# A hybrid decoder layer on one core: a longer count for an inversion, norm roots with their own rank, and one residual added by the transfer

## The chip, the core and the metric

The kernel runs on one core of a Trainium2 chip. The core has engines with instruction queues of their own: TensorE (PE in the profile) multiplies matrices into PSUM banks, VectorE (DVE) and ScalarE (ACT) work elementwise, GpSimd (POOL) and SyncE (SP) here issue transfers between DRAM and the core's memory. Each engine takes its instructions in the order in which the program has them, and an instruction waits on semaphores for what it reads and for the buffer that it writes. The metric is the device time of one execution in microseconds (us); lower is better.

## What is computed

One layer of a decoder, on 1024 positions of width 1024, in float32. Cut to what matters here:

```python
h = rms_norm(x, norm_mix_pre)
proj = h @ w_in                                # RWKV r,k,v and low ranks | S5 input u | two gates
g_rwkv, g_s5 = jnp.split(jax.nn.sigmoid(gates_of(proj) + b_gate), 2, axis=-1)
o_rwkv = rwkv7_branch(p_rwkv, ...) @ w_branch_rwkv   # delta-rule state, then a norm per head
o_s5 = s5_branch(u_s5, ...) @ w_branch_s5            # diagonal state space, GELU, GLU
mixed = (g_rwkv * o_rwkv + g_s5 * o_s5) @ w_out
x = x + rms_norm(mixed, norm_mix_post)         # the first residual
h = rms_norm(x, norm_ffn_pre)
f = conv_ffn(h, w_up, conv_w, conv_b, w_down)
x = x + rms_norm(f, norm_ffn_post)             # the second residual
```

`rms_norm` multiplies by the reciprocal root of the mean square over the 1024 channels.

## The kernel before

Activations lie transposed: channels on the 128 partitions, positions along the free axis, in tiles of 128x512. The 1024 positions are worked as two halves of 512 (`th` 0 and 1). Every float32 product is three matmuls on a split of both operands into a high and a low part (`mm3_steps`, lines 172 to 174: high by high, low by high, high by low); three such matmuls are a step. Splitting an operand takes ScalarE (the high part, lines 156, 226, 231) and VectorE (the low part, lines 157, 227, 232). Results collect in a few PSUM banks; two of them (`gm`) serve the wide products around the change.

**What sets TensorE's order.** TensorE's instructions stand in the order in which the code is written, and `drive` decides that order while the program is built. Lanes (generators) yield a cost and a delay in estimated us: `prep_lane` (the RWKV half's inputs, its Gram matrices and `rwkv_inv`, the inversion of its triangular blocks), `chain_lane` (`rwkv_level`, then the eight steps of `rwkv_chain` over the state), `out_lane` (`rwkv_out`: norm per head, transposes, gate). A lane that is not ready by the driver's own clock gives way to a stream of filling work (`fill`): `merge` for the first half (gates and GLU, eight tiles of one gate and eight of the other), then `merge_s5` (the S5 side of the second half), then the output projection of the first half, and behind the lanes the norms. The constant `T_INV` is the delay by which the driver counts VectorE's and the transfers' part of an inversion; `T_LN` and `T_LE` are those of the norm in `rwkv_out`, for the first and the second half. A longer delay lets more of the filling work go ahead of what waits, and takes it from what comes later.

**What sets the other engines' order.** VectorE, ScalarE, GpSimd and SyncE are ordered by a scheduler by rank: `high_priority(n)` ranks instructions earlier. `HPW` is used for loads of weights and gate tiles, and `HPN` above that.

**The level of the second half.** `rwkv_inv` ends on VectorE (lines 788, 790) and goes through DRAM and back on POOL's queue (`xd`, line 792; `gr`, line 797). `rwkv_level` transposes `gr` on VectorE (line 811, four instructions), multiplies on TensorE (line 821) and copies on ScalarE (line 825). Beside it run tiles of `merge`. Such a gate tile loads a 128x512 tile `GT` into one of three buffers `ev` (line 1184), makes 12 matmuls into `gm`, and multiplies both on VectorE (line 1192), which frees the `gm` bank; an add (line 1238) and a split (231, 232) free the `ev` buffer. `s5_inputs` (line 1243) loads a tile `YU` into the same three buffers (line 1166), with a Gelu (line 1167), and a cast and a subtraction (226, 227) behind it.

**The norm in `rwkv_out`.** For each of two groups VectorE subtracts a mean, sums squares (ScalarE squares into `ev` buffers for the second half, lines 912 and 913), makes a root (lines 131 to 139) and multiplies (line 916). TensorE transposes the result (line 922).

**The norms behind the mixing sublayer.** `mid_norms` sums squares of the projection's eight tiles `mx`, calls `post_norm` and then norms once more for the next sublayer. `rstd` makes a reciprocal root on VectorE out of nine small instructions (lines 265 and 131 to 139), `spread` brings it to all partitions by TensorE (line 271). `post_norm` loads x into buffers `tx` by SP, multiplies each tile by root and gain (line 1295), adds x (line 1296), squares the sum on ScalarE (line 257), adds up the squares on VectorE (line 259, first half) and stores the sum to DRAM (line 1299, from ScalarE's queue for the first half). At the same time the second half's `merge_rk` runs: its gate tiles load `GT` on POOL's queue (line 1184), and their products are split by lines 231 and 232.

Of the kernel before, what the change touches and what calls it, by code (L numbers as in the profile page):

```python
# [13 lines left out]
ALU = mybir.AluOpType  # L14
# [6 lines left out]
NK = D // 128  # L21
# [45 lines left out]
class Kern:  # L67
# [194 lines left out]
    def rstd(self, ss, eps, scale):  # L262

        v = self.small.tile([128, 4], F32, tag="rv", name=self.nm("rv"), bufs=2)
        self.nc.vector.tensor_scalar(v, ss[:, :4], scale, eps, ALU.mult, ALU.add)
        return self.rsqrt(v, 4, "nr")

    def spread(self, bc, y):

# [1009 lines left out]
    def post_norm(self, src, ss, th, gain, resid, store, squares=None):  # L1279


        nc = self.nc
        o = slice(th * 512, th * 512 + 512)
        xs, sq = [], []
        for k in range(NK):
            xs.append(self.tx())
            nc.sync.dma_start(xs[k], resid(k, o))
        bc = self.rp()
        y = self.rstd(ss, 1e-6, 1.0 / D)
        yield 0, T_RS  # L1290
        self.spread(bc, y)
        yield 0.9, 0
        for k in range(NK):
            y = src[k]
            nc.vector.scalar_tensor_tensor(y, y, self.vec(gain, k), bc, ALU.mult, ALU.mult)
            (nc.vector if k % 2 or squares is not None else nc.gpsimd).tensor_tensor(y, y, xs[k], ALU.add)
            if squares is not None:
                sq.append(self.square_into(sq[-1] if sq and th == 0 else None, y))
                (nc.sync if th else nc.scalar).dma_start(store(k, o), y)
            else:  # L1300
                (nc.sync if th else nc.gpsimd).dma_start(store(k, o), y)
        if squares is not None:
            yield 0, T_N2 if th else T_N5
            for i, x in enumerate(sq if th else sq[-1:]):
                self.sumsq(squares, x, i == 0)
                yield 0.5, T_N4

    def outproj(self, th, mg, mx):

# [556 lines left out]
    def prep_lane(self, g):  # L1866
        for th in range(2):
            yield 0, (lambda: self.masked >= 2 * th + 1 and self.all_in) if g else (lambda: self.chunks >= 14 * th)
            d = self.ds[th][g]
            self.rwkv_tiles(d, g, th)  # L1870
            yield from self.rwkv_front(d, g, th, self.pts[th], (lambda: self.chains >= 1) if th > g else (lambda: self.grams > 2 * th) if g else T_LD)
            self.fronts += 1
            if g:
                yield from self.rwkv_inv(self.ds[th], th)
                yield 0, T_INV
                self.preps += 1

    def chain_lane(self):
# [29 lines left out]
T_LD, T_SQ, T_LT = 6.0, 3.0, 3.5  # L1908
NEVA = 4
T_KN, T_BK, T_GR, T_NF, T_MT, T_INV, T_LV, T_CH = 7.0, 4.0, 4.0, 5.0, 8.0, 43.0, 1.0, 0.8  # L1910
T_LN, T_LE = 32.0, 20.0
T_N0, T_RS, T_N1, T_N2, T_N4, T_N5, T_N3 = 2.5, 4.0, 2.2, 5.0, 1.6, 40.0, 2.0
NET = 5
MGAP = 2
# [17 lines left out]
HPW, HPN = 400000, 500000  # L1932
# [64 lines left out]
```

## Time and profile before

| | |
|---|---|
| runs before | 1499.52, 1508.82, 1509.49 us; median 1508.82 |
| the profiled execution | 1501.13 us; its span 1499.4 us |
| TensorE's granted clock over that span | 0.98 of full |
| TensorE busy | 1436.3 us |
| VectorE, ScalarE busy | 1072.2 us, 730.3 us |
| bytes read and written in DRAM | 150.14 MB, 52.43 MB |

The span runs from the first to the last instruction that the profiler recorded; the execution's own time has the start and the end around it. A row of the timeline gives the start in us, the duration in us, the engine, the line of the code, the operation, the tile written and those read, the shape, and in brackets how long the engine stood idle before it and what ended that. `SPq` and `ACTq` are the queues of SyncE and ScalarE when they issue a transfer. In the list of waits a row reads: who waited for whom, us in total, times, longest.

### The profile page before, as it was taken

How to read it: one execution, taken by the hardware profiler on the slowest of the kernel's cores; microseconds unless marked ns; L12 is line 12 of the kernel's file. 1: busy time of each engine (PE TensorE's matmuls, PEld its weight loads, DVE VectorE, ACT ScalarE, POOL GpSimd, SP SyncE). 2: the span in 40 equal slices, each digit the busy share in tenths (PEclk: the TensorE clock that was granted, in tenths of full speed). 3: DMA queues.
4: the chain of work that ended last, by engine and by line, in shares of the span. 5: the costliest groups of instructions: out<-in, count | busy, mean ns of one | idle time of the engine just before them, and what ended most of it. 6: DMA issues, size and time to landing. Idle time of an engine off the chain costs nothing. (4 is left out here: it accounts for less than half of the span.)

```text
span 1499.4 us, 24150 instructions
## 1 busy us (share of the span) xinstructions
PE 1436.3 (96%) x9284; PEld 1177.0 (78%) x9284; DVE 1072.2 (72%) x1761; ACT 730.3 (49%) x1167; POOL 58.7 (4%) x116
## 2 busy tenths in 40 slices
PE   7999999999999899798999999999999999999996
PEld 5778888788878687576878877888888887888785
DVE  8977774756226859456597799777777777697677
ACT  7677653533324564443455455444444444444351
POOL 0000000010100110100000000000000000000001
PEclk9999999999999999799999999999999999999997
DMA  6453432642512675433365633222222227943723
GB/s 221 124 187 113 131 94 93 203 133 100 170 52 76 189 222 177 135 100 113 117 197 179 204 125 128 84 79 78 83 85 84 85 71 243 322 143 126 229 95 112
DMA packets 121284, 206.26 MB, mean 138 GB/s; under 512 B 29248, under 2 KB 35520, under 8 KB 121168
## 3 DMA queue, kind: packets, MB, share of 16 engines
q1 hardware_dynamic: 113296, 182.43, 37.7%
q0 software_dynamic: 6144, 19.99, 4.0%
q10 hardware_dynamic: 1728, 2.29, 0.4%
q8 instruction: 73, 1.20, 0.3%
q14 instruction: 43, 0.35, 0.1%
HBM read 150.14 MB, written 52.43 MB: 135 GB/s over the span
## 5 line engine op out<-in xcount | busy, mean ns | idle before, releaser
L172 PE MATMUL gm<-hh,wh 128*128 128x512 f32 x672 | 276.6, 412 | 8.0 <-DVE rsy L139 5.1
L173 PE MATMUL gm<-hl,wh 128*128 128x512 f32 x672 | 265.7, 395 | 0.0
L174 PE MATMUL gm<-hh,wl 128*128 128x512 f32 x672 | 265.3, 395 | 0.0
L156 ACT CAST wh<-wf 128x512 fp32r<-128x512 f32 x171 | 105.7, 620 | 186.3 <-PE gm L173 117.8
L157 DVE TENSOR_TENSOR wl<-wf,wh 128x512 fp32r<-128x512 f32 x171 | 117.0, 687 | 91.6 <-ACT wh L156 89.2
L172 PEld LDWEIGHTS gm<-hh,wh 128*128 128x128 f32 x672 | 127.9, 190 | 40.2 <-issue 7.9
L174 PEld LDWEIGHTS gm<-hh,wl 128*128 128x128 f32 x672 | 128.1, 191 | 28.1
L173 PEld LDWEIGHTS gm<-hl,wh 128*128 128x128 f32 x672 | 128.3, 191 | 25.1 <-issue 1.0
L1615 PE MATMUL d<-xl,wh 128*128 128x512 f32 x308 | 120.8, 392 | 3.5 <-DVE xl L227 3.5
L1614 PE MATMUL d<-xh,wh 128*128 128x512 f32 x308 | 120.9, 392 | 2.1 <-ACT xh L226 2.1
L1616 PE MATMUL d<-xh,wl 128*128 128x512 f32 x308 | 120.6, 392 | 0.0
L1440 PE MATMUL rp<-t,h 128*128 128x512 f32 x216 | 84.4, 391 | 2.6 <-ACT p L1454 1.6
L1442 PE MATMUL rp<-t,l 128*128 128x512 f32 x216 | 84.2, 390 | 0.5 <-DVE l L227 0.5
L1441 PE MATMUL rp<-t,h 128*128 128x512 f32 x216 | 84.1, 389 | 0.0
L1615 PEld LDWEIGHTS d<-xl,wh 128*128 128x128 f32 x308 | 58.2, 189 | 16.7 <-DVE xl L227 4.7
L1614 PEld LDWEIGHTS d<-xh,wh 128*128 128x128 f32 x308 | 58.2, 189 | 14.8 <-ACT xh L226 2.5
L1616 PEld LDWEIGHTS d<-xh,wl 128*128 128x128 f32 x308 | 58.1, 189 | 12.1
L226 ACT CAST h<-r 128x1024 fp32r<-128x1024 f32 x34 | 35.8, 1054 | 61.1 <-PE rp L1441 29.6
L227 DVE TENSOR_TENSOR l<-r,h 128x1024 fp32r<-128x1024 f32 x34 | 41.6, 1224 | 29.2 <-ACT h L226 27.7
L1461 DVE SCALAR_TENSOR_TENSOR y<-zv,vecs,y 128x1023 f32<-128x1023 f32 (+1 forms) x36 | 46.1, 1280 | 8.5 <-ACT y L1459 8.5
L1440 PEld LDWEIGHTS rp<-t,h 128*128 128x128 f32 x216 | 40.5, 188 | 12.2 <-ACT p L1454 2.5
L1454 ACT COPY p<-rp 128x512 f32<-128x512 f32 x54 | 31.0, 574 | 37.0 <-PE rp L1442 37.0
(459 smaller groups left out, 3198.5 us busy)
## 6 DMA issues: line engine op xcount, KB each, us to landing
r<-in_w_up_dram SPq DMA_DIRECT2D x36, 512.0 KB, 3.6
wf<-in_w_in_dram SPq DMA_DIRECT2D x62, 256.0 KB, 2.9
st<-in_w_down_dram SPq DMA_DIRECT2D x55, 256.0 KB, 4.1
st<-ACT SPq DMA_DIRECT2D x44, 256.0 KB, 4.4
wf<-in_w_up_dram SPq DMA_DIRECT2D x36, 256.0 KB, 2.6
ACT<-y POOLq DMA_DIRECT2D x18, 512.0 KB, 2.9
GT<-ev SPq DMA_DIRECT2D x32, 256.0 KB, 2.5
wf<-in_w_br_dram SPq DMA_DIRECT2D x32, 256.0 KB, 2.7
```

The lines of the kernel that those rows point to most:

```text
L156: nc.scalar.copy(h[:, :n], f[:, :n])
L157: nc.vector.tensor_tensor(l[:, :n], f[:, :n], h[:, :n].bitcast(F32), ALU.subtract)
L172: mm(ps, a, xh[k], start=k == 0, stop=False)
L173: mm(ps, a, xl[k], start=False, stop=False)
L174: mm(ps, b, xh[k], start=False, stop=k == n - 1)
L1440: mm(ps, wh[:, c], xh, start=first and k == 0, stop=False, skip_group_check=True)
L1441: mm(ps, wh[:, c], xl, start=False, stop=False, skip_group_check=True)
L1442: mm(ps, wl[:, c], xh, start=False, stop=k == 3, skip_group_check=True)
L1461: V.scalar_tensor_tensor(y[:, lag:], z[:, 0:1024 - lag], self.vec(nme, i), y[:, lag:], ALU.mult, ALU.add)
L1614: mm(ps, wh[:, c], xh[:, x], start=start, stop=False, skip_group_check=True)
L1615: mm(ps, wh[:, c], xl[:, x], start=False, stop=False, skip_group_check=True)
L1616: mm(ps, wl[:, c], xh[:, x], start=False, stop=stop, skip_group_check=True)
```

## The change

Three things:

1. The second half's inversion has a delay of its own, `T_INV2` = 50, where both had `T_INV` = 43, and `T_LE` goes from 20 to 16.
2. The instructions that `rstd` puts on VectorE get the rank `HPN`.
3. In `post_norm`, the first half no longer loads x into `tx` and adds it on VectorE. An accumulating transfer on POOL's queue adds x out of DRAM to the tile in place. The branches without squares go, which no caller used.

```diff
     def rstd(self, ss, eps, scale):
         v = self.small.tile([128, 4], F32, tag="rv", name=self.nm("rv"), bufs=2)
-        self.nc.vector.tensor_scalar(v, ss[:, :4], scale, eps, ALU.mult, ALU.add)
-        return self.rsqrt(v, 4, "nr")
+        with self.tc.high_priority(HPN):
+            self.nc.vector.tensor_scalar(v, ss[:, :4], scale, eps, ALU.mult, ALU.add)
+            return self.rsqrt(v, 4, "nr")
...
-        for k in range(NK):
+        for k in range(NK if th else 0):
             xs.append(self.tx())
             nc.sync.dma_start(xs[k], resid(k, o))
...
             nc.vector.scalar_tensor_tensor(y, y, self.vec(gain, k), bc, ALU.mult, ALU.mult)
-            (nc.vector if k % 2 or squares is not None else nc.gpsimd).tensor_tensor(y, y, xs[k], ALU.add)
-            if squares is not None:
-                sq.append(self.square_into(sq[-1] if sq and th == 0 else None, y))
-                (nc.sync if th else nc.scalar).dma_start(store(k, o), y)
+            if th:
+                nc.vector.tensor_tensor(y, y, xs[k], ALU.add)
             else:
-                (nc.sync if th else nc.gpsimd).dma_start(store(k, o), y)
+                nc.gpsimd.dma_start(y, resid(k, o), accum_op=ALU.add)
+            sq.append(self.square_into(sq[-1] if sq and th == 0 else None, y))
+            (nc.sync if th else nc.scalar).dma_start(store(k, o), y)
...
-                yield 0, T_INV
+                yield 0, T_INV2 if th else T_INV
...
-T_LN, T_LE = 32.0, 20.0
+T_LN, T_LE, T_INV2 = 32.0, 16.0, 50.0
```

From line 266 on, a line of the changed kernel has a number higher by one, up to the edit in `post_norm`. The numbers of this text are those of the kernel before unless it says otherwise.

**The level of the second half.** TensorE before, around the transposes that go ahead of the level (line 761; `gm_1153` and `gm_1171` are gate tiles of `merge`):

```order
L173 MATMUL gm_1153_6360<-hl_1122_6249,wh_1150_6354 128x512
L174 MATMUL gm_1153_6360<-hh_1121_6248,wl_1151_6355 128x512
L761 MATMUL rp_1154_6373<-csts_185,ld_962_5562 128x128 x4
L172 MATMUL gm_1171_6416<-hh_1082_6101,wh_1168_6410 128x512
L173 MATMUL gm_1171_6416<-hl_1083_6102,wh_1168_6410 128x512
L174 MATMUL gm_1171_6416<-hh_1082_6101,wl_1169_6411 128x512
```

TensorE now, around the same transposes (line 762; `gm_1186` is two gate tiles further on than `gm_1171`):

```order
L172 MATMUL gm_1186_6465<-hh_1095_6150,wh_1183_6459 128x512
L173 MATMUL gm_1186_6465<-hl_1096_6151,wh_1183_6459 128x512
L174 MATMUL gm_1186_6465<-hh_1095_6150,wl_1184_6460 128x512
L762 MATMUL rp_1187_6472<-csts_185,ld_962_5562 128x128 x4
L172 MATMUL gm_1186_6465<-hh_1108_6199,wh_1183_6459 128x512
L173 MATMUL gm_1186_6465<-hl_1109_6200,wh_1183_6459 128x512
```

Behind the transposes stood 18 matmuls of gate tiles ahead of the chain's first products (line 849), and 18 stand there now; 30 matmuls more have come ahead of the transposes. VectorE in the same place before, with the four transposes of the level (line 811, the last row two of them):

```order
L1192 SCALAR_TENSOR_TENSOR ev_1167_6408<-ev_1167_6408,gm_1171_6416 128x512
L1238 TENSOR_TENSOR ev_1167_6408<-ev_1167_6408,hl_1084_6105 128x512
L811 STREAM_TRANSPOSE ld_1155_6382<-gr_847_4905 32x512
L232 SCALAR_TENSOR_TENSOR hl_1173_6432<-ev_1167_6408,hh_1172_6431 128x512
L227 TENSOR_TENSOR hl_1177_6440<-ld_1175_6436,hh_1176_6439 128x512
L811 STREAM_TRANSPOSE ld_1155_6382<-gr_847_4905 32x512
L227 TENSOR_TENSOR hl_1190_6645<-ld_1188_6641,hh_1189_6644 128x512
L811 STREAM_TRANSPOSE ld_1156_6383<-gr_906_5254 32x512 x2
```

and now (line 812; line 1193 is the product of a gate tile, `gm_1186` the sixth, `gm_1204` the seventh tile of `merge`, which reads `GT14` through `ev_1200`):

```order
L1239 TENSOR_TENSOR ev_1182_6457<-ev_1182_6457,hl_1110_6203 128x512
L157 TENSOR_TENSOR wl_1249_6936<-wf_1250_6937,wh_1248_6935 128x512
L227 TENSOR_TENSOR hl_1181_6454<-ld_1179_6450,hh_1180_6453 128x512
L232 SCALAR_TENSOR_TENSOR hl_1195_6502<-ev_1182_6457,hh_1194_6501 128x512
L812 STREAM_TRANSPOSE ld_1188_6481<-gr_847_4905 32x512
L1193 SCALAR_TENSOR_TENSOR ev_1200_6513<-ev_1200_6513,gm_1204_6521 128x512
L227 TENSOR_TENSOR hl_1199_6510<-ld_1197_6506,hh_1198_6509 128x512
L1239 TENSOR_TENSOR ev_1200_6513<-ev_1200_6513,hl_1123_6252 128x512
L812 STREAM_TRANSPOSE ld_1188_6481<-gr_847_4905 32x512
L812 STREAM_TRANSPOSE ld_1189_6482<-gr_906_5254 32x512
L232 SCALAR_TENSOR_TENSOR hl_1208_6635<-ev_1200_6513,hh_1207_6634 128x512
L812 STREAM_TRANSPOSE ld_1189_6482<-gr_906_5254 32x512
```

The first transpose stood behind the product of the fourth tile, and now stands behind that of the sixth; the other three stand behind that of the seventh.

**The norm in `rwkv_out`, second half.** VectorE before, at the first group's root and product (`gm_1340` and `gm_1346` are the last two tiles of `merge_s5`, which read `GT14` and `GT15`):

```order
L138 SCALAR_TENSOR_TENSOR rsh_1324_7572<-rsh_1324_7572,lv_1320_7563 128x16
L136 SCALAR_TENSOR_TENSOR rsy_1329_7595<-rsh_1330_7596,rsy_1329_7595 128x16
L1192 SCALAR_TENSOR_TENSOR hl_1335_7622<-ev_1336_7623,gm_1340_7631 128x512
L139 SCALAR_TENSOR_TENSOR rsy_1323_7571<-rsh_1324_7572,rsy_1323_7571 128x16
L137 TENSOR_TENSOR rsh_1330_7596<-rsy_1329_7595 128x16
L916 TENSOR_TENSOR mt_1196_6663<-mt_1196_6663,rsy_1323_7571 128x1024
L1192 SCALAR_TENSOR_TENSOR hl_1341_7645<-ev_1342_7646,gm_1346_7654 128x512
```

and now (line 917 is the product):

```order
L137 TENSOR_TENSOR rsh_1336_7624<-rsy_1335_7623 128x16
L915 TENSOR_SCALAR lv_1338_7639<-lv_1338_7639 128x16
L138 SCALAR_TENSOR_TENSOR rsh_1336_7624<-rsh_1336_7624,lv_1332_7615 128x16
L131 TENSOR_SCALAR rsy_1341_7647<-lv_1338_7639 128x16
L139 SCALAR_TENSOR_TENSOR rsy_1335_7623<-rsh_1336_7624,rsy_1335_7623 128x16
L132 TENSOR_SCALAR rsy_1341_7647<-rsy_1341_7647 128x16
L917 TENSOR_TENSOR mt_1214_6731<-mt_1214_6731,rsy_1335_7623 128x1024
L157 TENSOR_TENSOR wl_1386_7826<-wf_1387_7827,wh_1385_7825 128x512
```

The two products of gate tiles have left the norm. On TensorE, `gm_1340` and `gm_1346` stood behind the chain's last matmuls (line 890); their like, `gm_1322` and `gm_1330`, stand inside the chain now but for the last six matmuls. Between the chain's last matmuls and the transposes of line 922 stood 96 matmuls of filling work, and 78 stand there now.

**The first norm behind the mixing sublayer.** ScalarE before, where the Squares (line 257) of the first tiles stand among the casts of the second half's products (line 231) and of weights (line 156):

```order
L257 ACTIVATE tm_1466_8182<-mx_1354_7705 128x512
L1299 DMA X1_115<-mx_1354_7705 128x512
L156 CAST wh_1510_8369<-wf_1512_8371 128x512
L231 ACTIVATE e_1480_8257<-et_1334_7613 128x512
L231 ACTIVATE hh_1487_8284<-et_1482_8261 128x512
L156 CAST wh_1513_8375<-wf_1515_8377 128x512
L257 ACTIVATE tm_1467_8187<-mx_1363_7746 128x512
L1299 DMA X1_115<-mx_1363_7746 128x512
L156 CAST wh_1519_8410<-wf_1521_8412 128x512
L231 ACTIVATE hh_1494_8311<-et_1489_8288 128x512
```

and now, each Square (line 257) reading a tile that an accumulating transfer has written:

```order
L257 ACTIVATE tm_1458_8166<-mx_1354_7705 128x512
L1302 DMA X1_115<-mx_1354_7705 128x512
L156 CAST wh_1502_8353<-wf_1504_8355 128x512
L257 ACTIVATE tm_1459_8171<-mx_1363_7746 128x512
L231 ACTIVATE e_1472_8241<-et_1346_7665 128x512
L1302 DMA X1_115<-mx_1363_7746 128x512
L257 ACTIVATE tm_1460_8177<-mx_1380_7814 128x512
L156 CAST wh_1505_8359<-wf_1507_8361 128x512
L231 ACTIVATE hh_1479_8268<-et_1474_8245 128x512
L1302 DMA X1_115<-mx_1380_7814 128x512
L231 ACTIVATE hh_1486_8295<-et_1481_8272 128x512
L156 CAST wh_1511_8394<-wf_1513_8396 128x512
```

The second and third Square have come ahead of the casts of `et_1346` and of all four `hh`. On POOL's queue the transfers of these three stand ahead of the load of `GT7`, and the other five behind it.

More of the change, by code (lines that the diff above doesn't have):

```diff
@@ L1295, in post_norm @@
             nc.vector.scalar_tensor_tensor(y, y, self.vec(gain, k), bc, ALU.mult, ALU.mult)
-            (nc.vector if k % 2 or squares is not None else nc.gpsimd).tensor_tensor(y, y, xs[k], ALU.add)
-            if squares is not None:
-                sq.append(self.square_into(sq[-1] if sq and th == 0 else None, y))
-                (nc.sync if th else nc.scalar).dma_start(store(k, o), y)
-            else:
-                (nc.sync if th else nc.gpsimd).dma_start(store(k, o), y)
[L1302 to L1306, printed above, removed]
+            if th:
+                nc.vector.tensor_tensor(y, y, xs[k], ALU.add)
+            else:
+                nc.gpsimd.dma_start(y, resid(k, o), accum_op=ALU.add)
+            sq.append(self.square_into(sq[-1] if sq and th == 0 else None, y))
+            (nc.sync if th else nc.scalar).dma_start(store(k, o), y)
+        yield 0, T_N2 if th else T_N5
+        for i, x in enumerate(sq if th else sq[-1:]):
+            self.sumsq(squares, x, i == 0)
+            yield 0.5, T_N4
     def outproj(self, th, mg, mx):
```

## The prediction

> **What bounds the kernel now.** I read the page first, then TensorE's waits, then stretches of the timeline around the longest of them, then the table by windows for the clock.
>
> ```profile
> span 1499.4 us, 24150 instructions
> PE 1436.3 (96%) x9284; PEld 1177.0 (78%) x9284; DVE 1072.2 (72%) x1761; ACT 730.3 (49%) x1167; POOL 58.7 (4%) x116
> ```
>
> TensorE is busy for 96% of the span, and the change leaves its instruction count as it is. So only what TensorE waits for, and what it loses by a lower clock behind a wait, can change. The rows of its waits that the change can touch:
>
> ```profile
> PE cz L821 <- DVE ld L811: 6.7, 2, 5.1
> PE gm L172 <- DVE rsy L139: 5.1, 1, 5.1
> PE rp L821 <- DVE ld L811: 3.9, 2, 3.6
> ...
> PE rp L271 <- DVE rsy L139: 2.1, 1, 2.1
> ```
>
> The L821 rows are the level of the second half, 6.7 + 3.9 = 10.6 us in one place. The second row is a gate tile that waits for a PSUM bank beside the norm of `rwkv_out`; the fourth is the spread of the first norm root behind the mixing sublayer. Behind two of these waits the clock falls too (columns: busy time of PE and its instructions, granted clock, DMA share, GB/s):
>
> ```profile
> 614.57:623.50 8.93, 5.44 (x12) 0.51 0.69 230
> 697.50:701.50 4.00, 4.00 (x10) 0.50 0.02 4
> 701.50:710.00 8.50, 8.50 (x38) 0.98 0.19 62
> ```
>
> The first row counts matmuls on `gm` alone. A wide matmul takes 8.50 / 38 = 0.224 us at clock 0.98 (0.227 between steady starts) and, with the first counted apart, 0.427 at clock 0.50. So the stall at the level costs 10.6 us and 12 x 0.20 = 2.4 us more, the one at 697.50 costs 5.06 and some ten slow matmuls, 10 x 0.20 = 2.1 us with the first one's 0.57.
>
> **Part 1: the second inversion counted at 50 for 43.** The driver puts 30 matmuls of gate tiles (10 steps, 30 x 0.227 = 6.8 us) ahead of the level. Nothing is added; the same 30 are missing further on. Before, TensorE ran out of them at 599.65 and stood until the transposes L811 came. What held these:
>
> ```profile
> 596.78 0.33 SPq L1184 DMA_DIRECT2D ev<-GT  x1
> ...
> 603.94 0.70 DVE L811 STREAM_TRANSPOSE ld<-gr 32x512 f32<-32x512 f32 x1 [1.69 <-DMA gr<-xd]
> ...
> 610.64 0.69 DVE L227 TENSOR_TENSOR hl<-ld,hh 128x512 fp32r<-128x512 f32 x1 [4.09 <-ACT hh L226]
> 611.25 1.43 DVE L811 STREAM_TRANSPOSE ld<-gr 32x512 f32<-32x512 f32 x2
> ...
> 613.71 0.32 SPq L1184 DMA_DIRECT2D ev<-GT  x1
> 614.57 0.80 PE L172 MATMUL gm<-hh,wh 128*128 128x512 f32 x1
> ```
>
> and, from the transfers issued between 595 and 615:
>
> ```profile
> ev<-GT SPq DMA_DIRECT2D x4, 256.0 KB, 4.1
> ```
>
> The first transpose came with its data, at 603.94. The last two came 7.3 us later, because VectorE takes its instructions in order and an L227 ahead of them waited 4.09 us for ScalarE's cast of a YU tile. The order of the changed kernel puts more ahead of them: the second to fourth transposes stand behind the product of the seventh gate tile (GT14), whose load is the seventh since 596.78 through three `ev` buffers. If each buffer turns at landing plus three VectorE instructions, 4.1 + 3 x 0.68 = 6.1 us, GT14 is issued at 596.78 + 2 x 6.1 = 609.0 where it was 613.71. Then landing 4.1, and six VectorE instructions up to the last transpose at some 0.63 each, 3.8; then the last 1.9 us of L821's matmuls: 618.8. At the other end GT14 gains nothing: 613.71 + 4.1 + 3.8 + 1.9 = 623.5. Before, the level ended at 614.57, and the 30 matmuls take it to 621.4 for equal work. So this part lies between a gain of 2.6 and a loss of 2.1 us. I take a gain of 1.5: the gate tiles' TensorE work comes earlier, so buffers are freed sooner than before, and the end is nearer to the first. The waits are not removed but moved: some stand at the `gm` bank of the sixth tile, the rest at the level. The slow clock behind them stays, and neither adds to the sum.
>
> **Part 2: the shorter latency behind the second chain (16 for 20), and the 30 matmuls gone.** Between the last L890 and the transposes L922 stood 96 fill matmuls, now 78; the two gate tiles with GT14 and GT15 of the S5 branch now run inside the chain. Before, they did this:
>
> ```profile
> 683.55 0.51 PE L890 MATMUL cz<-U,gr 64*64 64x64 f32 x11
> ...
> 692.14 0.33 SPq L1184 DMA_DIRECT2D ev<-GT  x1
> ...
> 696.67 0.68 DVE L1192 SCALAR_TENSOR_TENSOR hl<-ev,gm 128x512 f32<-128x512 f32 x1
> 697.47 1.23 DVE L916 TENSOR_TENSOR mt<-mt,rsy 128x1024 f32<-128x1024 f32 x1
> 697.50 0.77 PE L172 MATMUL gm<-hh,wh 128*128 128x512 f32 x1 [5.06 <-DVE rsy L139]
> ...
> 699.62 1.22 DVE L916 TENSOR_TENSOR mt<-mt,rsy 128x1024 f32<-128x1024 f32 x1
> ...
> 713.26 0.93 PE L922 MATMUL rp<-csts,mt 128*128 128x128 f32 x7
> ```
>
> SP loaded GT14 only at 692.14, since the norm's squares held the `ev` buffers; the product L1192 stood in the middle of the norm on VectorE; both PSUM banks were taken until then, so TensorE stood 5.06 us. With both products ahead of the norm the cause is gone: 5.06 + 2.1 = 7.2 us. The cover must hold: VectorE's norm delivered its first result at 697.47 + 1.23 = 698.7, 15 us after the chain's last matmuls, and 78 matmuls give 78 x 0.227 = 17.7 us. 2.7 us are left, and the two products no longer stand in the norm. Next in line is the second group's transposes, with 27 matmuls (6.1 us) between them and the first, against 2.2 us between the two L916. I take the whole 7.2; the other end is 0.
>
> **Part 3: roots ranked first.** The first root's last instruction moves up by one instruction of VectorE:
>
> ```profile
> 755.84 0.68 DVE L232 SCALAR_TENSOR_TENSOR e<-et,e 128x512 fp32r<-128x512 f32 x1
> 756.44 0.15 DVE L139 SCALAR_TENSOR_TENSOR rsy<-rsh,rsy 128x4 f32<-128x4 f32 x1
> ```
>
> One L232 less in front is 0.6 us of TensorE's 2.09. That L232 comes some 0.2 us later, and no wait of TensorE's hangs on it. The roots of the other norms move past rows whose readers are not waited for by TensorE. I take 0.5, between 0 and 1.
>
> **Part 4: the residual by accumulating transfers.** Removed: eight loads of x on SP, and eight adds on VectorE. Added: eight transfers of 256 KB on POOL's queue, on which ScalarE's Square and the store wait; three stand ahead of POOL's load of GT7. No such transfer is in the trace. VectorE was full here:
>
> ```profile
> 748.90:793.00 44.10, 42.01 (x191) 34.59 (x191) 42.03 (x76) 22.34 (x39) 2.15 (x4) 1.00 0.67 216
> ```
>
> ```profile
> L1296 DVE TENSOR_TENSOR mx<-mx,tx 128x512 f32<-128x512 f32 x8 | 5.5, 684 | 0.0
> ```
>
> (the stretch: busy time and instructions of PE, PEld, DVE, ACT and POOL, clock, DMA; then the adds as a group in it), and in order of time, with the nearest transfers' median landing last:
>
> ```profile
> 757.34 0.75 DVE L1295 SCALAR_TENSOR_TENSOR mx<-mx,vecs,rp 128x512 f32<-128x512 f32 x1 [0.74 <-PE rp L271]
> ...
> 763.67 0.54 POOL L1184 DMA_DIRECT2D et<-GT  x1 [6.32 <-DVE e L232]
> 765.58 0.63 ACT L231 ACTIVATE hh<-et 128x512 fp32r<-128x512 f32 x1 [1.11 <-DVE et L1275]
> 774.67 0.69 DVE L232 SCALAR_TENSOR_TENSOR hl<-et,hh 128x512 fp32r<-128x512 f32 x1
> 776.45 0.39 PE L173 MATMUL mm<-hl,wh 128*128 128x512 f32 x1
> 791.74 0.69 DVE L259 TENSOR_TENSOR tm<-tm,tm 128x512 f32<-128x512 f32 x1
> 797.30 0.94 PE L245 MATMUL rp<-ones,tm 128*128 128x1 f32 x8
> ```
>
> ```profile
> et<-GT POOLq DMA_DIRECT2D x8, 256.0 KB, 3.9
> ...
> xd<-mt POOLq DMA_DIRECT2D x2, 512.0 KB, 5.1
> ```
>
> The eight adds are 5.5 us of a full VectorE, but TensorE waited for none of them: 42.01 of 44.10 us it was busy, and 2.09 is the root's. So their removal gains nothing by itself. The price is at ScalarE: the first three Squares stand ahead of the casts that split the merged tiles (the first was at 765.58). By the order the first L1295 runs at 757.34 less the gain of part 3, and the third some 3.4 us on, with no add between: I take 760.75 for its end and the issue of the third transfer. Landing 4.5 us later the Squares are through before 765.9; later than that, each us holds the casts for a us, and the split used last had 776.45 - 775.36 = 1.1 us to spare, of which the two tiles' re-ordering takes most. The bounds: 3.9 us as for a plain load of this size on this queue, which costs 0; 5.1 us as for one of double size, about 0.8 us. An accumulation reads as many bytes again, so the second row is as near; I take 0.4. The other five have time: the sum of squares was ready at 792.4 and read at 797.30. Range 0 to +3 (a landing of 7.5).
>
> The Trainium skill speaks against this part (GPSIMD Engine Reference, section Key points): GpSimd shares its SBUF interfaces with VectorE and contends with instructions that have two SBUF inputs. By that, a full VectorE of tensor-tensor operations would delay the writing of descriptors. The trace does not bear it out for plain loads: POOL's load at 763.67 was issued in 0.54 us amid them.
>
> **Sum.** -1.5 - 7.2 - 0.5 + 0.4 = -8.8 us. The profiled execution took 1501.13 us (span 1499.4, and 1.7 around it), so its like would take 1492.3. That execution is 7.7 us under the median of 1508.82, and the three runs shown lie 10 us apart, so I put the difference to the median: 1500.0.
>
> **Rivals.**
> - The level is hidden altogether (chance 0.13). It needs VectorE's transposes within 603.9 to 607, before the 30 matmuls are through. For: the data were there at 603.94. Against: the order, which has the products of three gate tiles first. Part 1 would then give 10.6 + 2.4 = 13.0 us: 1508.8 - 20.3 = 1488.5.
> - The 5-us wait only moves (0.15): the gate tiles inside the chain wait for their loads, or the norm outlasts the 78 matmuls by being interleaved with more L157. Part 2 gives 0: about 1507.
> - The accumulating transfers hold ScalarE (0.08), which ends slower than before. From 4.5 us of landing each further us costs one, and about 2 us of slow clock once the wait passes 5 us; 9.2 us of gain are eaten at 4.5 + 9.2 - 2.0 = 11.7 us of landing, and at 16 us the time is 1513. For: ScalarE's queue is in order, and nothing of the trace has this transfer's duration. Against: the slowest 256-KB row on POOL's queue is 3.9.
> - VectorE blocks POOL (0.03): if descriptors are written late, each issue waits for at least one VectorE instruction of 0.69 us, three for 2.1 us, and ScalarE with them; about 1502, inside my range. The Trainium skill's GPSIMD Engine Reference (Key points) is the page that has such a contention.
>
> **Numbers.** The forecast has 0.61, and its own range is 1497 to 1506: -2.6 to +2.1 in part 1 and 0 to +3 in part 4 about the sum. The range to 1488 and 1510 takes in most of the first and all of the second rival, and leaves out the worse part of the third and an edge of the first. About 1% (15 us) is what a measurement of this kernel can tell from no change. Faster by over 1% needs under 1493.7: the first rival and an edge of the forecast, since runs differ by 10 us, 0.20. Slower by over 1% needs over 1523.9: a landing of 27 us by the same sum, or what I have not seen, 0.04. Within 1%: 0.76.
>
> **What would show it.** Part 1: waits for L812 that end at 619 to 622. Part 2: no wait over 1 us between the last L891 and L923, and clock 0.98 or more there. Part 3: a wait at L271 of about 1.5 us. Part 4: eight accumulating transfers that land in 4 to 5 us, and TensorE without a wait over 1 us between 757 and 800 of the old span. Wrong would make it: a Square that waits over 5 us, a first L923 that waits for L917, or a level that ends before 616.

## The result, and the profile after

| | before | changed |
|---|---|---|
| median (range) of six runs, us | 1505.66 (1499.52 to 1509.49) | 1494.02 (1488.83 to 1497.15) |
| ratio, 95% interval | | 0.9926 [0.9902, 0.995] |
| the profiled execution, us | 1501.13 | 1494.83 |
| its span, us | 1499.4 | 1493.1 |

The changed kernel is faster by 0.74%, between 0.5% and 1.0%. Measured once more, with ten runs of it and fifteen of the kernel before, the ratio was 0.9951 [0.9932, 0.997]. The two profiled executions lie 6.3 us apart. The page of the changed kernel, span and busy time by engine:

```profile
span 1493.1 us, 24165 instructions
...
PE 1432.7 (96%) x9284; PEld 1172.1 (79%) x9284; DVE 1067.4 (71%) x1753; ACT 729.6 (49%) x1167; POOL 66.0 (4%) x124
```

VectorE has eight instructions less and POOL eight more. These rows of TensorE's waits answer to the four of the prediction, and one is new:

```profile
PE cz L822 <- DVE ld L812: 7.6, 2, 4.6
...
PE gm L172 <- DVE ev L1193: 2.1, 1, 2.1
...
PE mm L173 <- DVE hl L232: 1.8, 2, 1.5
...
PE rp L272 <- DVE rsy L139: 1.4, 1, 1.4
```

The 5.1-us wait at a gate tile is not in the list any more. The waits at the level stand there as 7.6 + 2.1 = 9.7 us, where they were 10.6. The third row is new, and lies in the output projection of the second half, behind the first norm root.

**Where the time went between these two executions.** The timeline of both gives the starts of a few landmarks. Kernel before (in its line numbers):

```profile
499.21 2.37 PE L681 MATMUL rp<-csts,gr 128*128 128x2 f32 x16 [0.92 <-DVE ld L735]
...
612.73 1.91 PE L821 MATMUL rp<-ld,gr 32*32 32x32 f32 x62 [0.36 <-DVE ld L811]
```

The changed kernel at the same places, and on to the places that the prediction showed of before:

```profile
501.26 1.92 PE L682 MATMUL rp<-csts,gr 128*128 128x2 f32 x16 [0.92 <-DVE ld L736]
...
617.51 0.28 PE L822 MATMUL cz<-ld,gr 32*32 32x32 f32 x2 [4.62 <-DVE ld L812]
620.82 1.86 PE L822 MATMUL cz<-ld,gr 32*32 32x32 f32 x61 [3.02 <-DVE ld L812]
...
624.70 0.80 PE L172 MATMUL gm<-hh,wh 128*128 128x512 f32 x1
...
691.35 0.51 PE L891 MATMUL cz<-U,gr 64*64 64x64 f32 x11
...
709.62 1.03 PE L923 MATMUL rp<-csts,mt 128*128 128x128 f32 x8
...
749.58 0.65 PE L272 MATMUL rp<-csts,rsy 128*128 128x128 f32 x4 [1.38 <-DVE rsy L139]
...
794.44 0.95 PE L245 MATMUL rp<-ones,tm 128*128 128x1 f32 x8
```

From one landmark to the next, with 0.227 us taken off for each fill matmul that the order has more (30 ahead of the level) or added for each that it has less (18 behind the chain):

| stretch | before | changed | difference |
|---|---|---|---|
| start to L681 of the second half | 499.2 | 501.3 | +2.1 |
| from there to the level's end | 115.4 | 123.4 - 6.8 = 116.6 | +1.2 |
| level's end to the chain's last L890 | 69.0 | 66.7 | -2.3 |
| from there to L922 | 29.7 | 18.3 + 4.1 = 22.4 | -7.3 |
| the root (its wait) | 2.09 | 1.38 | -0.7 |
| spread of the root to the sum of squares | 40.65 | 44.86 | +4.2 |
| the FFN, rows that the change doesn't touch | 602.3 | 599.2 | -3.1 |

The level's end is the start of the first wide matmul behind it (614.57 before, 624.70 now), and the chain's end the start of its last eleven L890 (683.55 and 691.35). The other 12 of the 30 matmuls are missing between L922 and the root, where the two kernels otherwise take the same time. The first and the last row are not the change's. In the thirteen profiles of this study the first stretch took 499.1 to 501.4 us, with and without the change's parts, and the FFN 599 to 606. These two stretches together differ by up to 7 us from one profile to another, and runs of one kernel lie some 10 us apart. So parts of some us are read here from stretches of the profile and not from run times.

### The profile page after: what moved, and what is told of

The parts are those of the page before. It is cut to its first block, busy times and chain, and to the rows that moved or that the text cites. A ratio compares the mean times of both kernels' runs of the same rounds, so it can differ in the third digit from the quotient of the medians.

```text
span 1493.1 us, 24165 instructions
## 1 busy us (share of the span) xinstructions
PE 1432.7 (96%) x9284; PEld 1172.1 (79%) x9284; DVE 1067.4 (71%) x1753; ACT 729.6 (49%) x1167; POOL 66.0 (4%) x124
## 5 line engine op out<-in xcount | busy, mean ns | idle before, releaser
L157 DVE TENSOR_TENSOR wl<-wf,wh 128x512 fp32r<-128x512 f32 x171 | 117.1, 687 | 79.6 <-ACT wh L156 76.8
L1440 PEld LDWEIGHTS rp<-t,h 128*128 128x128 f32 x216 | 40.5, 188 | 11.1 <-ACT p L1454 2.4
```

The lines of the kernel that those rows point to most:

```text
L157: nc.vector.tensor_tensor(l[:, :n], f[:, :n], h[:, :n].bitcast(F32), ALU.subtract)
L1440: mm(ps, wh[:, c], xh, start=first and k == 0, stop=False, skip_group_check=True)
```

## Experiments

Each ran on one chip with the kernel before. A ratio is to the kernel before, with its 95% interval.

**The parts alone.** First the change without its accumulating transfers, `x1`:

```diff
-                nc.gpsimd.dma_start(y, resid(k, o), accum_op=ALU.add)
+                nc.vector.tensor_tensor(y, y, xs[k], ALU.add)    # and the loads of xs, as before
```

> The changed kernel with the residual of the first half loaded and added on VectorE again; both counts and the rank stay. Theory A (the accumulating transfers hold ScalarE at the Square, 1.8 us of waits of TensorE and some 2.4 us of slow clock behind them): no wait over 0.3 us between the spread of the first root and the sum of squares, clock 1.00 there, and about 4 us less than the changed kernel, so about 15 us (1.0%) below the kernel before, ratio 0.990. Theory B (the waits there come from the ranked root or from gate tiles that now come earlier, not from the transfers): the wait of 1.5 us stays, and the time is that of the changed kernel, ratio 0.9926, or above.

Measured: 1492.88 us median, ratio 0.9936 [0.9915, 0.9957]. Its timeline at the two ends of the stretch:

```profile
746.28 0.65 PE L272 MATMUL rp<-csts,rsy 128*128 128x128 f32 x4 [1.36 <-DVE rsy L139]
...
786.94 0.95 PE L245 MATMUL rp<-ones,tm 128*128 128x1 f32 x8
```

Between spread and sum of squares lie 40.66 us, as before the change, and no wait. So the waits there come from the transfers; theory B falls. The ratio of 0.990 that theory A gave did not come: in run times the transfers cannot be told from nothing, 0.9936 against 0.9926 and 0.9951.

`x2` is the kernel before with the transfers alone.

> The kernel before with the accumulating transfers alone. Theory A: three Squares wait for their transfers, about 5 us in sum, TensorE waits 1.5 to 2 us in the output projection of the second half and runs at half clock for 3 us or so: 4 us slower than before, ratio 1.003. Theory B: eight adds less on a full VectorE and nothing else: 0 to 2 us faster, ratio 0.999 to 1.000.

Measured: 1503.3 us, ratio 1.0005 [0.999, 1.0019]: no gain, and no loss that can be measured. Its stretch is 804.61 - 761.87 = 42.74 us, 2.1 more than before, but with one wait of 0.21 us alone. The rest is another thing (windows; clock in the column behind PE's busy time):

```profile
752.00:759.00 7.00, 7.00 (x37) 1.00 0.54 148
759.00:762.00 3.00, 0.93 (x5) 1.00 0.79 259
762.00:765.50 3.50, 3.50 (x12) 0.57 0.57 169
765.50:772.00 6.50, 6.50 (x29) 0.97 0.93 191
```

Behind the root's wait of 2.08 us TensorE ran at about half its clock for 3.5 us, eight matmuls of 0.43, before the first of these transfers could be waited for. That is 8 x 0.20 = 1.6 us, and it leaves 0.5 for the transfers. Their loss may have been small here because the slow stretch gave ScalarE time; that isn't shown. The interval leaves out theory A's 1.003 and takes in theory B's 1.000.

`x3` has both counts alone (the two `T_` edits of the diff), `x4` the rank alone (`with self.tc.high_priority(HPN)` in `rstd`).

> The kernel before with both counts alone (50 for the second inversion, 16 for the norm's latency). Theory A: the 5-us wait beside the norm is gone with its slow clock (7.2 us) and the level gains 1 to 2 us with waits of about 2, 4.6 and 3 us: 8 to 9 us faster, ratio 0.994. Theory B (the counts shift the level's waits without gain, and the gain of the changed kernel comes from the rank or the transfers too): 5 to 7 us, ratio 0.996.

> The kernel before with the rank of the norm roots alone. Theory A: the wait at the spread of the first root falls from 2.1 to 1.4 us, all else stays: 0.7 us faster, which is within the measurement, ratio 0.9995. Theory B (moving the roots delays rows in front of other waits; the changed kernel's profile ran 2.4 us late by 570 us of its span): the start of the profile is 1 to 2.5 us late, time 1 to 2 us slower, ratio 1.001.

Measured: `x3` 1495.63 us, ratio 0.9954 [0.9938, 0.997]; `x4` 1499.82 us, 0.9986 [0.9971, 1.0002]. `x3` has no wait over 1 us between chain and norm, as theory A has it, and 2.45, 4.05 and 2.64 us of waits at the level. Its level ended 1.1 us later than before for equal work, not 1 to 2 us sooner, and its ratio lies between the two theories. In `x4` the root's wait is 1.42 us, and its start to L681 took 500.42: no delay that the changed kernel doesn't share with kernels without the rank (`x2`: 501.41). Counts, rank and transfers sum to 0.9954 + 0.9986 + 1.0005 - 2 = 0.9945, which agrees with the whole.

**Which count ends the 5-us wait.** `x8` has the inversion's count alone, `x9` the norm's:

```diff
-                yield 0, T_INV                          # x8
+                yield 0, T_INV2 if th else T_INV        # x8: T_INV2 = 50, T_LE = 20
-T_LN, T_LE = 32.0, 20.0                                 # x9
+T_LN, T_LE = 32.0, 16.0                                 # x9
```

> The kernel before with the second inversion counted at 50 alone; the norm's latency stays at 20. Theory A (the 30 matmuls moved ahead of the level take the two S5 gate tiles out of the norm, and that ends the 5-us wait): no wait over 1 us between the chain's end and the transposes behind the norm, 7 us less from there to the first norm behind the mixing sublayer; time as with both counts, ratio 0.9954. Theory B (the shorter latency ends it): the 5-us wait stays, ratio 0.999.

> The kernel before with the norm's latency counted at 16 alone. Theory A: the 5-us wait at the gate tile stays as it is, and with 18 matmuls less ahead of the transposes (78 for 96) nothing new waits, since the norm ends 17.7 + 5 us before: same time, ratio 1.000. Theory B: the wait is gone, 7 us faster, ratio 0.995; or the transposes come too early and wait 1 to 2 us for the norm, ratio 1.001.

Measured: `x8` 1494.17 us, ratio 0.9943 [0.9921, 0.9965]; `x9` 1502.77 us, 1.0009 [0.9992, 1.0026]. The row of `x9` at the gate tile:

```profile
697.01 0.77 PE L172 MATMUL gm<-hh,wh 128*128 128x512 f32 x1 [5.06 <-DVE rsy L139]
```

and TensorE in `x8` between chain and transposes:

```profile
694.00:716.00 22.00, 22.00 (x121) 1.00 0.45 144
```

The inversion's count does it all: 30 matmuls earlier, the last two S5 gate tiles are out of the norm's way (in `x8` the last of their products on VectorE starts at 697.19, ahead of the norm's squares and root). The norm's shorter count alone leaves the wait to its hundredth. Behind the longer inversion it adds nothing that these runs can tell.

**What holds the level.** `x5` is `x1` with the level's transposes ranked:

```diff
-                V.transpose(xz[lo[h]]...)
+                with self.tc.high_priority(HPN):
+                    V.transpose(xz[lo[h]]...)
```

> Both counts and the rank of the roots, the residual on VectorE as before, and the level's four transposes ranked with the roots, so that they stand together behind the product of the sixth gate tile and ahead of the seventh's. Theory A (VectorE's order holds the level, not the data): the waits of 5.0 and 3.1 us at the level fall to 3 us or less in sum, and the time from the first matmul behind the inversion to the level's end shrinks by 5 us: about 4 to 6 us less than the same kernel without this rank, ratio 0.990. Theory B (the wait is for the gate tiles' loads through three buffers, and the transposes only change places with it): the wait moves to the seventh gate tile or to the chain behind the level, gain under 1 us, ratio 0.9936.

Measured: 1489.54 us (1480.1 to 1495.36), ratio 0.9905 [0.9877, 0.9933], the fastest kernel of the study. VectorE in the changed kernel at the level:

```profile
613.06 0.69 DVE L1193 SCALAR_TENSOR_TENSOR ev<-ev,gm 128x512 f32<-128x512 f32 x1 [2.23 <-DMA ev<-GT]
...
616.67 0.69 DVE L812 STREAM_TRANSPOSE ld<-gr 32x512 f32<-32x512 f32 x1
618.14 0.69 DVE L1193 SCALAR_TENSOR_TENSOR ev<-ev,gm 128x512 f32<-128x512 f32 x1 [0.77 <-DMA ev<-GT]
...
620.06 1.43 DVE L812 STREAM_TRANSPOSE ld<-gr 32x512 f32<-32x512 f32 x2
...
622.10 0.70 DVE L812 STREAM_TRANSPOSE ld<-gr 32x512 f32<-32x512 f32 x1
```

and in `x5`:

```profile
609.43 0.69 DVE L1194 SCALAR_TENSOR_TENSOR ev<-ev,gm 128x512 f32<-128x512 f32 x1 [1.46 <-DMA ev<-GT]
...
611.84 2.89 DVE L813 STREAM_TRANSPOSE ld<-gr 32x512 f32<-32x512 f32 x4
614.76 0.69 DVE L1194 SCALAR_TENSOR_TENSOR ev<-ev,gm 128x512 f32<-128x512 f32 x1
```

With the transposes as one block ahead of the seventh gate tile, the level ended 5.4 us sooner than in `x1` (117.1 against 122.5 us behind L681). Its waits fell from 8.1 to 3.3 us beside the one for the `gm` bank, which was 2.31 us and became 2.81. So VectorE's order held most of the level: theory A. Some 2.4 us were lost again right behind it, since the clock stayed low for longer:

```profile
616.50:625.40 8.90, 8.90 (x140) 0.50 0.48 156
```

From L681 to the transposes behind the norm the net is 3.0 us (204.3 against 207.3). The intervals of the ratios of `x5` and `x1` overlap, so it is the profile that shows this gain and not the run times.

`x10` adds a fourth `ev` buffer to `x5` (`NEV = 4`, and `NLD = 9` for 10 to make room).

> The kernel with the level's transposes ranked and the residual on VectorE, and a fourth buffer for the gate and YU tiles (one of ten buffers of another pool given up for it). Theory A (three buffers pace the loads: the wait of 2.8 us for a gm bank and 3.3 us at the level both end with a gate tile's load): both waits fall to 3 us in sum or less, another 3 to 5 us, ratio 0.987. Theory B (what is left is ScalarE's and VectorE's order, or the inversion's data): 5 us or more of waits stay, ratio 0.990 to 0.991; or the buffer given up makes a wait of its own behind the chain, ratio above 0.991.

Measured: 1492.32 us, ratio 0.9938 [0.9917, 0.9958]. The wait for the `gm` bank is gone (0.24 us), as theory A has it for that half. But the order changed with the buffer: the product of the seventh tile came to stand between the second and third transpose, and the level's waits rose to 4.4 + 2.9 = 7.3 us. VectorE there:

```profile
611.46 1.43 DVE L813 STREAM_TRANSPOSE ld<-gr 32x512 f32<-32x512 f32 x2
...
615.56 0.69 DVE L1194 SCALAR_TENSOR_TENSOR ev<-ev,gm 128x512 f32<-128x512 f32 x1 [1.96 <-DMA ev<-GT]
616.17 0.69 DVE L813 STREAM_TRANSPOSE ld<-gr 32x512 f32<-32x512 f32 x1
```

The third transpose stood behind a product that waited for its load. So both theories have a part of it: the three buffers made the bank's wait, the order the level's. The ratio is above those of both theories, and the profile has no new wait behind the chain that the buffer given up could have made. A fourth buffer with the transposes kept together wasn't tried.

**The transfers.** `x6` takes the first three of the eight back to VectorE (`for k in range(NK if th else 3)` for the loads, and the add where `th or k < 3`).

> The changed kernel, but the first three tiles of the residual are loaded by SP and added on VectorE again; the last five come by accumulating transfers. Theory A (only the first three hold ScalarE in front of the casts that the output projection waits for): no wait over 0.3 us of TensorE between the spread of the first root and the sum of squares, 40.7 us between them, and the time of the kernel without any such transfer, ratio 0.9936. Theory B (the last five matter too, or the slow clock comes from the root's wait alone): 42 to 45 us between them, ratio as the changed kernel's or above.

Measured: 1492.4 us, ratio 0.9936 [0.9916, 0.9956]; the stretch 40.90 us, no wait over 0.3. The last five cost TensorE nothing, though ScalarE waited 10.2 us for them in sum, and saving five adds on VectorE gained nothing that these runs can tell.

`x7` has plain loads in their place, issued and waited for alike (`accum_op=ALU.add` left out).

> The changed kernel with the eight transfers of the residual as plain loads over the tile, without the addition, so that its first half holds x alone behind the norm (the sum is left out); queue, issue and waits are the same. Theory A (adding makes the transfer itself slower, since it also reads what it writes): the plain loads land in 3 to 4 us where the adding ones took 4.1 to 10.5, median 6.6; ScalarE waits under 3 us for the first three, and TensorE has no wait over 0.5 us between the first root's spread and the sum of squares. Theory B (the time is that of a full DMA, which the weight loads share): they land in 5 us or more, and TensorE waits 1.5 us or more as in the changed kernel.

Measured: 1493.29 us, one execution. The stretch is 790.41 - 749.72 = 40.69 us, without a wait. ScalarE's first three Squares in the changed kernel:

```profile
757.21 0.63 ACT L257 ACTIVATE tm<-mx 128x512 f32<-128x512 f32 x1 [3.09 <-DMA mx<-in_x_dram]
...
760.24 0.63 ACT L257 ACTIVATE tm<-mx 128x512 f32<-128x512 f32 x1 [1.89 <-DMA mx<-in_x_dram]
...
761.62 0.63 ACT L257 ACTIVATE tm<-mx 128x512 f32<-128x512 f32 x1 [0.23 <-DMA mx<-in_x_dram]
```

and in `x7`:

```profile
755.08 0.63 ACT L257 ACTIVATE tm<-mx 128x512 f32<-128x512 f32 x1 [0.80 <-DMA mx<-in_x_dram]
757.17 0.63 ACT L257 ACTIVATE tm<-mx 128x512 f32<-128x512 f32 x1 [0.17 <-DMA mx<-in_x_dram]
759.56 0.63 ACT L257 ACTIVATE tm<-mx 128x512 f32<-128x512 f32 x1 [1.24 <-DMA mx<-in_x_dram]
```

The list of transfers issued between 745 and 800 us gives number, size and median us from issue to landing; changed kernel first, then `x7`:

```profile
mx<-in_x_dram POOLq DMA_DIRECT2D x8, 256.0 KB, 6.6
```

```profile
mx<-in_x_dram POOLq DMA_DIRECT2D x8, 256.0 KB, 4.5
```

Adding makes them 2 us slower in the median at the same place in the program (4.1 to 10.5 us against 3.0 to 6.8), and POOL's issue of one 0.86 to 1.31 us against 0.54. Theory A holds, though the plain loads also took longer than its 3 to 4.

`x11` is the changed kernel once more.

> The changed kernel unaltered, for a second profile and more runs. Theory A: the waits for the accumulating transfers come back with 40.7 + 2 to 4.5 us between the first root's spread and the sum of squares, and the part of it that is slow clock varies; ratio 0.993 within 0.002. Theory B: the wait of the first profile was an accident of that execution, and 41 us or less stand there.

Measured: 1494.42 us, ratio 0.9951 [0.9932, 0.997]; the stretch 790.26 - 748.33 = 41.93 us, with waits of 0.41 and 0.24 us and no half clock. So the wait comes back, but smaller than theory A had it (42.7 us or more), and above theory B's 41. Its price varies: 1.3 us here, 4.2 in the first profile, where it grew to 1.54 us and a slow stretch followed (770.69 us on, TensorE):

```profile
770.69 0.50 PE L173 MATMUL mm<-hl,wh 128*128 128x512 f32 x1 [1.54 <-DVE hl L232]
...
771.89 0.79 PE L173 MATMUL mm<-hl,wh 128*128 128x512 f32 x1 [0.23 <-DVE hl L232]
...
772.91 0.63 PE L172 MATMUL ch<-e,wh 128*128 128x512 f32 x1
```

## Why the prediction came out as it did

**The sum.** Forecast was 8.8 us less; the first comparison gives 0.74% of 1505.66, 11.1 us (7.5 to 14.8), the second 7.4 (4.5 to 10.2). Between the two profiled executions, the changed stretches up to the root give 1.2 - 2.3 - 7.3 - 0.7 = -9.1 us against -9.2 forecast (1.5 + 7.2 + 0.5), and the transfers +4.2 against +0.4; that leaves -4.9. With the second profile of the changed kernel (`x11`) it is -8.0. That the first parts agree so well is in part luck, as part 1 shows. The median, 1494.02, lies below the forecast's own 1497 to 1506 about 1500.0, though within the range to 1488: the forecast started from the median of three runs, 1508.82, and six gave 1505.66. The step that was most wrong is the landing of the transfers in part 4.

**Part 1, the level: the sum was right, the reason was not.** The forecast was that the end of the level gains 1.5 us and that the slow clock behind it stays. The level ended 1.2 us later for equal work, and over all profiles with the longer count and without the ranked transposes or the fourth buffer it did so by 0.7 on the mean (seven profiles, 116.5, against four, 115.8). The term that was mis-sized is the turn of a buffer: the `GT` loads took 5.0 us in the median and not 4.1 (changed kernel, transfers issued between 595 and 625 us),

```profile
ev<-GT SPq DMA_DIRECT2D x5, 256.0 KB, 5.0
```

and GT14 was issued at 614.38 of that profile, 15.2 us behind GT11 where the sum had 12.2. The gain came from what the forecast held fixed: from the level's end to the chain's end it took 66.5 to 66.8 us in six of those seven profiles and 69.0 to 70.4 in three of the four others (66.8 in the fourth, 69.9 in the seventh). The matmuls there are the same 150 wide ones in all of them; the difference is the clock. Behind the level it stayed at half for 8.8 us before and 3.8 us in the changed kernel (TensorE, first before, then changed; clock behind the count):

```profile
614.57:623.38 8.81, 8.81 (x142) 0.50 0.69 228
```

```profile
624.70:628.45 3.75, 3.75 (x42) 0.50 0.00 0
```

At half speed the 5.0 us between them cost 2.5, which is about the 2.3 measured. Why the clock came back sooner in most profiles of the new order isn't settled; `x8` has the new order and 11.4 us of half clock there, `x9` the old one and 3.5. So that this part came out near its 1.5 us is luck.

That VectorE's order would hold the level, and that the rival of a level hidden altogether fails on it, was right: `x5` took 5.4 us off the level's end by that order alone, and still had 3.3 us of waits.

**Part 2, the 5-us wait: right.** Forecast 7.2, measured 7.3, and TensorE has no wait over 0.1 us there. The cover of 78 matmuls held. But the forecast gave both counts a share, and `x8` and `x9` show that the inversion's count does it alone. The rival of a wait that only moves did not come.

**Part 3, the root: right, and too small.** 2.09 became 1.38 us. What was left out is the clock behind that wait: at 2.08 to 2.09 us it fell to half in three of five profiles (`x2`, `x3`, `x9`, for 3.41 us or 5 to 8 matmuls; not in the kernel before nor in `x8`), at 1.35 to 1.42 us in none of eight. That is worth up to 1.6 us more, and fits `x4`'s ratio of 0.9986, though its interval reaches past 1.

**Part 4, the transfers: the step that failed.** The prediction took 4.5 us as the landing up to which nothing waits, and a landing between 3.9 and 5.1 us. The mechanism was the one it described: ScalarE in order, the first three Squares ahead of the casts, about one us for each us of landing past that point, and then a slow clock. The size was not: the third transfer was issued at 754.47 and landed 7.1 us later (its Square began at 761.62), and the first took 5.8. By the prediction's own rule that is 7.1 - 4.5 = 2.6 us, without slow clock, since the rule has that only once the wait passes 5 us. Measured were 4.2: the clock fell behind a wait of 1.54 us already, and 3.41 us at half clock cost 1.7 of the 4.2 (an estimate, half of 3.41), which leaves 2.5. In `x11` the third landed in 6.15 us, which is 1.65 by the rule, and 1.3 were measured. So two things were mis-sized, the landing and the wait at which the clock falls. The rival of held transfers was the right mechanism at a smaller landing than the one from which it decides.

The rival by which VectorE delays POOL did not show: in `x7`, amid the same VectorE work, the issue of a plain load took the same 0.54 us all eight times:

```profile
L1300 POOL DMA_DIRECT2D mx<-in_x_dram x8: 536/536/536, 751.5 to 774.1; - x8
```

This is where the Trainium skill (GPSIMD Engine Reference, section Key points) has contention with VectorE instructions that read two SBUF inputs; no run here shows it for these transfers. The issues of the accumulating transfers differ among themselves, but each took the same time to 0.02 us in the changed kernel, `x11` and `x2` (0.91, 0.87, 1.10 us for the first three), which speaks against a wait for VectorE there too.

## What to carry to other kernels

A delay in a driver's table that lets filling work go ahead can end a wait far behind the place it is written for; look at which tiles the shift takes out of a later crowded stretch. When work is moved off an engine that is full, ask first whether anyone waits for that engine: here 5.5 us of adds were worth nothing, and the transfers that replaced them held another in-order queue. An instruction for which TensorE waits can wait less with a rank of its own on a crowded engine, as with the root and above all the level's transposes: counts, ranked roots and ranked transposes without the accumulating transfers (`x5`) gave 0.9905 [0.9877, 0.9933].

## What had not been expected of the hardware

- The clock fell to half behind a wait of 2.08 us in some executions and not in others. In each of the thirteen traces all changes of the granted clock lie whole multiples of 3.413 us apart, and a stretch at half clock lasts 3.41, 6.83, 10.24 us and so on (the last, cut off by the trace's end, aside). If these steps run on between the changes, the wait lay inside one step in the three profiles where the clock fell, and across the border of two in the two others. `x2`, with a fall, and `x8`, without, step by step (TensorE busy, clock behind the count):

```profile
759.06:762.47 3.41, 1.33 (x9) 1.00 0.81 264
762.47:765.88 3.41, 3.41 (x10) 0.50 0.56 148
```

```profile
748.16:751.57 3.41, 2.73 (x13) 1.00 0.82 192
751.57:754.99 3.42, 2.03 (x11) 1.00 0.73 270
754.99:758.00 3.01, 3.01 (x15) 1.00 0.43 126
```

  How much idle time in a step is enough isn't settled: in the kernel before 1.47 us busy of a step brought no fall, and in the changed kernel 1.72 (768.40 to 771.81) did.
- The Trainium skill (TensorE: Matmul & The Clock Gate, Part 1) puts the fall behind at least one idle window of about 3.4 us, on a window that runs free. That the outcome varies between executions, on steps of 3.413 us, agrees; that a wait of 2.08 us with full work before it was enough does not.
- Behind the level's end, TensorE worked without a wait for 3.4 us (`x11`) to 12.0 us (`x4`) before the full clock came back.
- An accumulating transfer of 256 KB on POOL's queue took 0.86 to 1.31 us to issue and 6.4 to 7.3 us in the median to land (changed kernel, `x11` and `x2`), against 0.54 and 4.5 for a plain load in its place (`x7`).
